# A four-layer decoder trunk on one core: attention steps reordered, low halves of weights moved from GpSimd to VectorE, and the last layer's down products turned

## The chip, the cores and the metric

The kernel runs on one core of a Trainium2 chip. A core has a matrix engine (TensorE), three engines for everything else (VectorE, ScalarE, GpSimd), a fifth one (SyncE) that only issues transfers, and DMA engines that move data between the chip's memory (HBM) and the core's working memory (SBUF). TensorE's results go to eight banks of accumulators (PSUM), from which VectorE and ScalarE read. The metric is the device time of one execution, in microseconds (us).

## The reference

A trunk of four pre-norm residual layers works on 256 tokens of 1024 features, in float32. Each layer adds a token mixer, then a SwiGLU feed-forward step with 2816 hidden features; a last RMS norm with its own gain ends it.

```python
for i in range(4):
    h = h + mixer[i % 3](rms_norm(h, norm_mix[i]))
    a = rms_norm(h, norm_ffn[i])
    h = h + (silu(a @ w_gate[i]) * (a @ w_up[i])) @ w_down[i]
return rms_norm(h, norm_final)
```

Layers 0 and 3 use native sparse attention (NSA): 16 query heads in 4 groups; keys and values exist in three kinds (for compressed blocks, for selected blocks, for a window). With 256 tokens every block is selected and the window reaches over all tokens, so the second and third kind are two full causal attentions. The compressed kind runs its keys and values through a small network (two products with a GELU between) and has 15 blocks. The three results are weighted by sigmoid gates, projected from the same input, and summed. Layer 1 uses MoBA, which with one block of 256 tokens is plain causal attention with 16 heads. Layer 2 is a gated convolution over three tokens between two projections.

## The kernel before

**Precision.** Matrix products run in a rounded float32 form. A number is split in two: a high half (a copy rounded to that form, `whi` for weights) and a low half (the number minus its high half, `wlo`). A product is three matmuls: high by high, high by low, low by high (`mm3`, L132 to L137; `group_wide` L139 does the first two at once with 512 columns, L155, and the third with 256, L159).

**The weight stream.** `stream()` (L884) lists all weights in the order in which the steps use them, and `tiles` packs them on the host into parts of eight 128x128 tiles (512 KB). `take` (L118) hands out tiles in that order and makes the parts ahead: up to five parts, the current one included (`AHEAD`), are loaded (four buffers `raw`), and split by `split_part` (L94) into five buffers each of `whi` and `wlo`. ScalarE makes the high half in one copy (L111). The low half is one subtraction of 128x1024 on VectorE or four of 128x256 on GpSimd (L115). Which engine makes it is written in the table `LO` (L42): a word per step, read cyclically by the part's number, `v` for VectorE, `p` for GpSimd. Steps that are not in the table, the convolution and the feed-forward steps among them, use VectorE. The weights of the compression network (step `F`) are used whole, in plain float32, and loaded straight into a `whi` buffer.

**The mixers as lists of steps.** `NSA_ORDER` and `MOBA_ORDER` (L39 to L41) are words that `steps` (L396) calls one by one. A, K, q, k: projections with the features on the partitions (A: four at once, raw compressed keys and values; K: keys; each `project`, L255, of 24 matmuls per 128 features). G: projection of the gates, which are transposed to tokens on the partitions right away (`put_gates`, L541, L545). V: values with tokens on the partitions (`values`, L359, 48 matmuls of 512 columns for each call). F, E, C, D: compression, its GELU, its keys and values. c, t: compressed scores with their softmax, and their transposes. For each pair of heads s, T, P: scores (L698 in NSA, L444 in MoBA) and softmax (`softmax`, L377: row minima `mn` of the negated, masked scores on VectorE L386, exponentials on ScalarE L389, division and gate on GpSimd L393), transposes (L718, L459) with a split of the result (`split`, L182: high half on ScalarE L184, low half on VectorE L185), and the products with the values (L735, L473). Step numbers count up unless a number is written.

**Accumulators.** The eight banks are three pools: A with four, B with three, C with one. Projections, values and scores use A (a pair of NSA heads takes three), transposes B.

**Feed-forward.** `ffn` (L285) has the tokens on the partitions for gate and up (L345 to L347), turns the hidden rows over 32x32 transposes on VectorE (L304) and small transfers, and splits them (L321). `out_proj` (L268) then computes the down products (and the mixers' output projections) with features on the partitions, four tiles of 128 features at once and then four single ones, adds them to `h` (L275, L276), and prepares the next norm: `prep` (L188) scales by the gain and splits, squares on ScalarE (L211) and sums squares on GpSimd (L213). The norm's factor is applied later, from sums that TensorE makes (`rms_sums` L226) and a power on GpSimd (`rms_tokens` L234, L239).

**The end.** For the last norm (number 8) `prep` makes rows scaled by the final gain, `turn_rows` (L217, L223) transposes them on TensorE beside the down products, and `run` scales them by the norm's factor (L871, L873) and stores four pieces of 128x512 over SyncE's queue (L874).

**Order on the engines.** The program is written on tiles; the framework's planner decides each engine's order of instructions from the written order, as priorities, and its own estimate of when things are ready, and sets the waits.

## Time and profile before

| | us |
|---|---|
| median of 3 runs | 1271.21 (1270.64 to 1273.55) |
| profiled execution | 1274.58 |
| its span, first instruction to last | 1272.8 |
| TensorE busy | 1239.8 |
| VectorE, ScalarE, GpSimd busy | 861.0, 686.5, 334.0 |
| mean granted TensorE clock, share of 2.4 GHz | 0.995 |

In the rows, PE is TensorE (PEld its weight loads), DVE VectorE, ACT ScalarE, POOL GpSimd, SPq SyncE's queue; L115 is line 115 of the kernel. Matmuls overlap: one of 512 columns is shown with some 390 ns, while the next may start earlier, so a stretch is read by its count and length. A releaser (`<-`) is what ended an engine's idle time. For GpSimd the kernel's lines show as one row where an instruction follows the other (x8: eight of them).

### The profile page before, as it was taken

What the parts mean: (1) busy time and instruction counts of PE and PEld (TensorE: products, weight loads), DVE (VectorE), ACT (ScalarE), POOL (GpSimd) and SP (SyncE); (2) the same over time, 40 slices, a digit from 0 to 9 for tenths busy, and PEclk for the clock granted to TensorE, in tenths of its full rate; (3) what the DMA queues carried; (4) which work ended last, traced back from release to release, by engine and by line L of the source; (5) the groups of instructions that cost most, each with busy time, mean ns of one, the idle gap of its engine ahead of it and who ended that gap; (6) DMA issues with size and microseconds to landing.
All of it is one profiled execution on the core that took longest, in us unless ns stands there. A gap on an engine that the chain in (4) does not pass through costs nothing.

```text
span 1272.8 us, 20178 instructions
## 1 busy us (share of the span) xinstructions
PE 1239.8 (97%) x7108; PEld 1082.7 (85%) x7108; DVE 861.0 (68%) x1621; ACT 686.5 (54%) x1231; POOL 334.0 (26%) x492
## 2 busy tenths in 40 slices
PE   8998999999998999999999999999999989999997
PEld 8977888888898888888899988888899878888886
DVE  7578785665648785656758786565746797756663
ACT  5578754554456754545434444454446796545542
POOL 3577610000467310000113110000346865000011
PEclk9999999999999999999999999999999999999999
DMA  8732166767554336776665656776655312677761
GB/s 278 244 110 64 42 208 199 243 198 228 181 180 124 112 120 197 232 212 205 222 189 171 199 183 196 216 220 213 205 183 199 115 36 69 205 221 217 227 210 51
DMA packets 91445, 226.73 MB, mean 178 GB/s; under 512 B 17488, under 2 KB 38352, under 8 KB 91344
## 3 DMA queue, kind: packets, MB, share of 16 engines
q1 hardware_dynamic: 91200, 225.41, 57.0%
q8 instruction: 56, 0.92, 0.3%
q14 instruction: 45, 0.37, 0.1%
q10 hardware_dynamic: 144, 0.04, 0.0%
HBM read 212.81 MB, written 1.05 MB: 168 GB/s over the span
## 4 chain that ended last, share of the span: by engine, by line
PE 85%; DVE 6%; ACT 4%; issue 3%; POOL 1%; DMA 0%; POOLq 0%; SPq 0%; DVEq 0%; ACTq 0%
PE psA L155 15%; PE psA L159 8%; PE psB L345 6%; PE psB L347 6%; PE psB L346 6%; PE psA L346 5%; PE psA L345 5%; PE psA L347 5%; PE psA L135 4%; PE psA L136 4%; PE psA L137 4%; PE psB L581 2%; PE psB L155 2%; PE psC L347 2%; PE psC L345 2%
## 5 line engine op out<-in xcount | busy, mean ns | idle before, releaser
L111 ACT CAST whi<-raw 128x1024 fp32r<-128x1024 f32 (+1 forms) x390 | 405.2, 1040 | 451.4 <-PE psC L347 97.4
L115 DVE TENSOR_TENSOR wlo<-raw,whi 128x1024 fp32r<-128x1024 f32 (+1 forms) x338 | 410.9, 1221 | 265.2 <-ACT whi L111 246.2
L155 PE MATMUL psA<-ff,whi 128*128 128x512 f32 x840 | 228.5, 393 | 0.0
L213 POOL TENSOR_TENSOR ssq<-ssq,row 128x256 f32<-128x256 f32 x48 | 45.7, 951 | 546.9 <-issue 398.6
L115 POOL TENSOR_TENSOR wlo<-raw,whi 128x256 fp32r<-128x256 f32 x208 | 157.8, 792 | 61.8 <-ACT whi L111 52.0
L155 PEld LDWEIGHTS psA<-ff,whi 128*128 128x128 f32 x840 | 149.4, 189 | 23.9
L135 PE MATMUL psA<-at,whi 128*128 128x256 f32 x536 | 153.9, 287 | 0.0
L137 PE MATMUL psA<-at,wlo 128*128 128x256 f32 x536 | 152.9, 285 | 0.0
L136 PE MATMUL psA<-at,whi 128*128 128x256 f32 x536 | 152.7, 285 | 0.0
L345 PE MATMUL psB<-whi,at 128*128 128x512 f32 x352 | 137.4, 390 | 0.0
L347 PE MATMUL psB<-whi,at 128*128 128x512 f32 x352 | 137.0, 389 | 0.0
L346 PE MATMUL psB<-wlo,at 128*128 128x512 f32 x352 | 136.9, 389 | 0.0
L159 PEld LDWEIGHTS psA<-ff,wlo 128*128 128x128 f32 x840 | 123.1, 190 | 10.9
L159 PE MATMUL psA<-ff,wlo 128*128 128x256 f32 x840 | 129.7, 282 | 0.0
L136 PEld LDWEIGHTS psA<-at,whi 128*128 128x128 f32 x536 | 103.6, 193 | 0.6
L135 PEld LDWEIGHTS psA<-at,whi 128*128 128x128 f32 x536 | 103.6, 193 | 0.5
L137 PEld LDWEIGHTS psA<-at,wlo 128*128 128x128 f32 x536 | 103.5, 193 | 0.0
L345 PE MATMUL psA<-whi,at 128*128 128x512 f32 x256 | 99.6, 389 | 0.0
L346 PE MATMUL psA<-wlo,at 128*128 128x512 f32 x256 | 99.6, 389 | 0.0
L347 PE MATMUL psA<-whi,at 128*128 128x512 f32 x256 | 99.6, 389 | 0.0
L389 ACT ACTIVATE pr<-pr,mn 128x128 f32<-128x128 f32 (+1 forms) x160 | 71.4, 450 | 13.7 <-DVE mn L386 12.8
L347 PEld LDWEIGHTS psB<-whi,at 128*128 128x128 f32 x352 | 66.1, 188 | 13.9
(214 smaller groups left out, 2037.6 us busy)
## 6 DMA issues: line engine op xcount, KB each, us to landing
raw<-in_w SPq DMA_DIRECT2D x384, 512.0 KB, 4.2
pt<-pt SPq DMA_DIRECT2D x320, 32.0 KB, 3.0
wf<-in_w SPq DMA_DIRECT2D x16, 512.0 KB, 4.3
h<-in_xt SPq DMA_DIRECT2D x4, 256.0 KB, 5.3
raw<-in_w SPq DMA_DIRECT2D x4, 256.0 KB, 5.3
pt<-pt SPq DMA_DIRECT2D x64, 16.0 KB, 3.1
out<-ff SPq DMA_DIRECT2D x4, 256.0 KB, 2.5
w<-in_w SPq DMA_DIRECT2D x2, 256.0 KB, 3.8
```

Of the source, the lines that this page charges most:

```text
L111: nc.scalar.copy(hi[:, c], src[:, c])
L115: eng.tensor_tensor(out=lo[:, d], in0=src[:, d], in1=hi[:, d].bitcast(F32), op=OP.subtract)
L135: mm(out, wt[0], act[0], start=first, stop=False)
L136: mm(out, wt[0], act[1], start=False, stop=False)
L137: mm(out, wt[1], act[0], start=False, stop=last)
L155: mm(outs[o], w[0], acts[k].rearrange("p i s -> p (i s)"), start=(k == 0), stop=(k == n - 1))
L159: mm(outs[o][:, :S], w[1], acts[k][:, 0, :], start=False, stop=False)
L213: (nc.gpsimd if norm else nc.vector).tensor_tensor(out=self.ssq, in0=self.ssq, in1=sq, op=OP.add)
L345: mm(o, a[:, 0, s], hi, start=(k == 0), stop=False)
L346: mm(o, a[:, 0, s], lo, start=False, stop=False)
L347: mm(o, a[:, 1, s], hi, start=False, stop=(k == KT - 1))
L389: nc.scalar.activation(pr[:, c], pr[:, c], AF.Exp, bias=mn[:, j:j + 1], scale=-1.0, accum_out=den[:, j:j + 1])
```

## The change

Both lists of steps have another order, and a new step `g` holds the transposes of the gates, apart from their projection. `LO` keeps four entries; a second table, `HI`, puts some high halves on VectorE (`a` is ScalarE). The low half of the NSA keys' second copy moves from GpSimd to VectorE. In the last layer `finish` takes the place of `out_proj`: tokens on the partitions, four banks for all 1024 features, the residual brought in by products with the identity, the final gain broadcast over the partitions and applied by VectorE, squares summed by ScalarE out of the banks, and two queues for the stores. Of the last four feed-forward tiles each bank is finished by itself, token half by token half. The stream then holds this layer's down weights by rows of 1024. `PROJ_BANKS` and `PR` carry the values that stood in the code before; the host's layout adds the broadcast gain and drops it from the table of gains.

```diff
@@ -36,14 +36,18 @@
 ROW_BUFS = 7
 PT_BUFS = 5
 PS_BUFS = {"A": 4, "B": 3, "C": 1}
-NSA_ORDER = ("A K0 q K3 F q F K1 F q F E G K2 q C c0 s D q s T t0 V q s T P q P s T P q T s "
-             "c1 s P T t1 s P T s P T P T P").split()
-MOBA_ORDER = ("V0 k k V1 q q k k s s q q T s k q s P T k T P q s P T q q P T k s T k s P s P T T P P").split()
-LO = {"V": "vp", "q": "vp", "nsa_out": "p", "moba_out": "vvvp", "G": "vvp", "K": "vp", "A": "vp", "moba_q": "p", "moba_V": "vp", "moba_k": "vvvp"}
-PIECES = 4
+NSA_ORDER = ("A q K q F K3 F F K1 F E G K g q q D C c s q s V t T q P s T q s P T q T c s s P T P s t P s T T "
+             "P T P P").split()
+MOBA_ORDER = ("k V k k q q q s s V T q k s s P k T q k T P q s q P T q P T k s k T s s P T P P T P").split()
+LO = {"nsa_out": "p", "moba_out": "vp", "G": "p", "A": "p"}
+HI = {"A": "v", "G": "ava", "K": "ava", "moba_out": "v"}
 OUT_BANKS = "AAAB"
 CMP_BANK = "B"
 GELU = "vector"
+PIECES = 4
+PROJ_BANKS = "AABB"
+PR = ["gpsimd"]
+KEY_LO = ["vector", "vector"]
 CONE = "vector"
 NPAIR = 8
 NCMP = 15
...
@@ -103,12 +107,13 @@
         src = self.raw.pop(q)
         hi = self.operands.tile([P, PART * P], F32R, tag="whi", name=f"whi{q}", bufs=W_BUFS)
         lo = self.operands.tile([P, PART * P], F32R, tag="wlo", name=f"wlo{q}", bufs=W_BUFS)
-        lo_eng = LO.get(self.names[q], "v")
+        lo_eng, hi_eng = (e.get(self.names[q], d) for e, d in ((LO, "v"), (HI, "a")))
         eng = {"p": nc.gpsimd, "v": nc.vector}[lo_eng[q % len(lo_eng)] if q >= 4 else "v"]
+        copy = {"a": nc.scalar.copy, "v": nc.vector.tensor_copy}[hi_eng[q % len(hi_eng)] if q >= 4 else "a"]
         n = PART * P // (2 if q < 4 else 1)
         for o in range(0, PART * P, n):
             c = slice(o, o + n)
-            nc.scalar.copy(hi[:, c], src[:, c])
+            copy(hi[:, c], src[:, c])
             m = n // (PIECES if eng is nc.gpsimd else 1)
             for b in range(o, o + n, m):
                 d = slice(b, b + m)
...
@@ -192,17 +197,11 @@
         g = self.gain[:, norm, k:k + 1]
         if k == 0:
             self.at = [None] * KT
-            self.scaled_rows = []
             self.ssq = None
-        if norm < 8:
-            a = self.operands.tile([P, 2, S], F32R, tag="at", name=self.uid("at"), bufs=8)
-            nc.vector.tensor_scalar(a[:, 0, :], h, g, None, op0=OP.mult)
-            nc.vector.scalar_tensor_tensor(a[:, 1, :], h, g, a[:, 0, :].bitcast(F32), op0=OP.mult, op1=OP.subtract)
-            self.at[k] = a
-        else:
-            hg = self.row()
-            nc.vector.tensor_scalar(hg, h, g, None, op0=OP.mult)
-            self.scaled_rows.append(hg)
+        a = self.operands.tile([P, 2, S], F32R, tag="at", name=self.uid("at"), bufs=8)
+        nc.vector.tensor_scalar(a[:, 0, :], h, g, None, op0=OP.mult)
+        nc.vector.scalar_tensor_tensor(a[:, 1, :], h, g, a[:, 0, :].bitcast(F32), op0=OP.mult, op1=OP.subtract)
+        self.at[k] = a
         if k == 0:
             self.ssq = self.sb([P, S], "ssq", bufs=1)
             nc.scalar.activation(self.ssq, h, AF.Square)
...
@@ -214,18 +213,9 @@
         else:
             self.sq = sq
 
-    def turn_rows(self, k):
-
-        if k == 0:
-            self.turned = [[self.bank(c) for _ in range(NT)] for c in "AB"]
-        for t in range(NT):
-            c = slice(k % 4 * P, (k % 4 + 1) * P)
-            self.nc.tensor.transpose(self.turned[k // 4][t][:, c], self.scaled_rows[k][:, t * P:(t + 1) * P],
-                                     self.ident)
-
     def rms_sums(self):
         nc = self.nc
-        pt = self.sums = self.bank("C" if self.norm == 8 else "A" if self.norm % 2 else "B")
+        pt = self.sums = self.bank("A" if self.norm % 2 else "B")
         for t in range(NT):
             c = slice(t * P, (t + 1) * P)
             nc.tensor.matmul(pt[:, t:t + 1], self.ssq[:, c], self.ones, start=True, stop=False)
...
@@ -276,9 +266,6 @@
                 self.nc.vector.tensor_tensor(out=h, in0=p[:, S:], in1=h, op=OP.add)
             for i in range(n):
                 self.prep(m + i, norm)
-            if norm == 8:
-                for k in range(max(m - 4, 0), m + n - 4):
-                    self.turn_rows(k)
             m += n
 
 
...
@@ -348,7 +335,60 @@
             if self.rstd is None:
                 self.rms_tokens()
             hidden(banks, n)
-        self.out_proj(hs, norm + 1)
+        (self.out_proj if norm < 7 else self.finish)(hs, norm + 1)
+
+
+    def finish(self, hs, norm):
+        nc = self.nc
+        mm = nc.tensor.matmul
+        g = self.sb([P, D], "pt", bufs=PT_BUFS)
+        nc.sync.dma_start(g, self.ap["gfin"])
+        banks = [[self.bank(c) for _ in range(2)] for c in "AB"]
+        for t in range(NT):
+            for k in range(KT):
+                mm(banks[t][k // 4][:, k % 4 * P:(k % 4 + 1) * P], self.h[k][:, t * P:(t + 1) * P], self.ident,
+                   start=(k % 4 == 0), stop=False, skip_group_check=True)
+
+        def products(t, k, halves, w):
+            s = slice(t * P, (t + 1) * P)
+            for hf in halves:
+                o, (hi, lo) = banks[t][hf], w[hf]
+                mm(o, hs[k][:, 0, s], hi, start=False, stop=False, skip_group_check=True)
+                mm(o, hs[k][:, 0, s], lo, start=False, stop=False, skip_group_check=True)
+                mm(o, hs[k][:, 1, s], hi, start=False, stop=(k == FT - 1), skip_group_check=True)
+
+        ss = self.sb([P, 2 * NT], "ss", bufs=1)
+
+        def scale(t):
+            xs = []
+            for hf in range(2):
+                x, y = (self.sb([P, 512], "pr", bufs=PR_BUFS) for _ in range(2))
+                nc.scalar.activation(x, banks[t][hf], AF.Square, accum_out=ss[:, 2 * t + hf:2 * t + hf + 1])
+                nc.vector.tensor_tensor(out=y, in0=banks[t][hf], in1=g[:, hf * 512:(hf + 1) * 512], op=OP.mult)
+                xs.append(y)
+            v, r = self.sb([P, 1], "var"), self.sb([P, 1], "rstd")
+            nc.vector.tensor_tensor(out=v, in0=ss[:, 2 * t:2 * t + 1], in1=ss[:, 2 * t + 1:2 * t + 2], op=OP.add)
+            nc.vector.tensor_scalar(v, v, 1.0 / D, EPS, op0=OP.mult, op1=OP.add)
+            nc.gpsimd.tensor_tensor(out=r, in0=v, in1=self.mhalf[:, :1], op=OP.pow)
+            for hf, y in enumerate(xs):
+                o = self.ff([P, 512], F32)
+                if hf:
+                    nc.scalar.activation(o, y, AF.Identity, scale=r)
+                else:
+                    nc.vector.tensor_scalar(o, y, r, None, op0=OP.mult)
+                (nc.scalar if hf else nc.sync).dma_start(self.ap["out"][t * P:(t + 1) * P, hf * 512:(hf + 1) * 512], o)
+
+        cut = FT - 4
+        for k in range(cut):
+            w = [self.take(4) for _ in range(2)]
+            for t in range(NT):
+                products(t, k, range(2), w)
+        ws = [[self.take(4) for _ in range(2)] for _ in range(cut, FT)]
+        for t in range(NT):
+            for hf in range(2):
+                for k in range(cut, FT):
+                    products(t, k, [hf], ws[k - cut])
+            scale(t)
 
 
     def scaled(self, p):
...
@@ -531,16 +571,20 @@
                     r, o = slice(i * DH, (i + 1) * DH), slice((1 - i) * DH, (2 - i) * DH)
                     nc.scalar.copy(kk[r, 0, b, :], f[r])
                     nc.scalar.copy(kk[o, 0, b, :], f[r])
-                    for eng, d in ((nc.vector, r), (nc.gpsimd, o)):
+                    for eng, d in zip((getattr(nc, e) for e in KEY_LO), (r, o)):
                         eng.tensor_tensor(out=kk[d, 1, b, :], in0=f[r], in1=kk[r, 0, b, :].bitcast(F32),
                                           op=OP.subtract)
             return put
 
         gates = self.sb([P, NT, 48], "gates", bufs=1)
 
+        scaled = []
+
         def put_gates(p):
-            f = self.scaled(p)
-            pg = self.bank("B")
+            scaled.append(self.scaled(p))
+
+        def turn_gates(_):
+            f, pg = scaled[0], self.bank("B")
             for t in range(NT):
                 nc.tensor.transpose(pg[:, t * P:(t + 1) * P], f[:, t * P:(t + 1) * P], self.ident)
             nc.scalar.activation(gates, pg[:, :S].rearrange("p (t c) -> p t c", t=NT)[:, :, 80:], AF.Exp, scale=-1.0)
...
@@ -857,21 +901,6 @@
             if i == 0:
                 self.pad_keys()
             self.ffn(2 * i + 1)
-        self.begin(8)
-        for k in range(4, KT - 1):
-            self.turn_rows(k)
-        self.rms_sums()
-        self.turn_rows(KT - 1)
-        self.rms_tokens()
-        for t in range(NT):
-            for hf in range(2):
-                o = self.ff([P, 512], F32)
-                src, r = self.turned[hf][t], self.rstd[:, t:t + 1]
-                if hf:
-                    nc.scalar.activation(o, src, AF.Identity, scale=r)
-                else:
-                    nc.vector.tensor_scalar(o, src, r, None, op0=OP.mult)
-                nc.sync.dma_start(ap["out"][t * P:(t + 1) * P, hf * 512:(hf + 1) * 512], o)
         assert self.pos == self.nblk * PART
 
 
...
@@ -916,7 +945,10 @@
         for g in range(0, FT, 4):
             n = min(4, FT - g) * P
             s.append(("ffn", "ffn_gate_up", i, np.concatenate([r(g * P, n), r(DFF + g * P, n)])))
-        s += out("ffn_w_down", i, "down")
+        if i < LAYERS[-1]:
+            s += out("ffn_w_down", i, "down")
+        else:
+            s.append(("down", "ffn_w_down", i, r(0, D)))
     return s
 
 
```

## Rows read from the trace of the kernel before

**Rows 1.** The page's busy times, TensorE's and its weight loads' lines.

```profile
PE 1239.8 (97%) x7108; PEld 1082.7 (85%) x7108; DVE 861.0 (68%) x1621; ACT 686.5 (54%) x1231; POOL 334.0 (26%) x492
```

**Rows 2.** Busy time by stage (stretch from:to in us from the span's start and its length, then busy us and instructions of each engine, the mean granted TensorE clock as a share of 2.4 GHz, the share of time that the DMA engines were busy, GB/s): first layer's attention and the head of its output projection, second layer's attention, short convolution, fourth layer's attention, last feed-forward stage and end; and TensorE's first matmul in order of time (start, length, engine, line, operation, out<-in, shapes, count, idle time before it and what ended it).

```profile
0.00:149.00 149.00, 135.12 (x938) 121.56 (x939) 112.45 (x342) 107.94 (x284) 90.47 (x147) 0.99 0.45 149
...
346.00:454.00 108.00, 103.77 (x679) 93.20 (x678) 70.79 (x168) 68.70 (x156) 59.39 (x93) 0.98 0.45 139
...
651.00:721.00 70.00, 70.00 (x586) 70.00 (x585) 52.47 (x84) 27.84 (x32) 17.24 (x22) 1.00 0.61 180
...
925.00:1066.00 141.00, 133.31 (x948) 120.68 (x947) 98.39 (x309) 101.11 (x268) 88.21 (x136) 0.99 0.37 120
1066.00:1273.00 207.00, 199.59 (x1000) 169.48 (x998) 126.91 (x175) 93.01 (x123) 21.13 (x25) 0.99 0.60 185
...
5.81 1.22 PE L177 MATMUL psA<-at,whi 128*128 128x256 f32 x4 [5.81 <-ACT whi L111]
```

**Rows 3.** TensorE's instructions in order of time at its longer stalls (columns as in the last row above; the bracket holds the idle time and its releaser).

```profile
56.97 0.44 PE L545 MATMUL psB<-ident,row 128*128 128x128 f32 x2 [0.81 <-DVE row L356]
...
109.40 0.73 PE L742 MATMUL psC<-pt,ff 128*128 128x512 f32 x1 [2.06 <-ACT pr L389]
...
403.58 0.47 PE L451 MATMUL psA<-keys,ff 128*128 128x512 f32 x1 [1.03 <-DVE mn L386]
...
411.51 0.33 PE L466 MATMUL psB<-ident,pr 128*128 128x128 f32 x1 [2.19 <-DVE pt L185]
...
974.21 0.44 PE L545 MATMUL psB<-ident,row 128*128 128x128 f32 x2 [0.81 <-DVE row L356]
...
996.71 0.60 PE L369 MATMUL psA<-whi,at 128*128 128x512 f32 x1 [1.81 <-DVE mn L386]
...
1027.30 0.47 PE L742 MATMUL psC<-pt,ff 128*128 128x512 f32 x1 [1.35 <-ACT pr L389]
```

**Rows 4.** Busy time of three stretches that begin with a long stall (columns as by stage; the share behind POOL is the granted clock).

```profile
107.00:115.00 8.00, 5.94 (x31) 5.28 (x31) 7.10 (x33) 5.68 (x19) 5.10 (x10) 0.79 0.24 68
411.00:419.00 8.00, 7.44 (x41) 6.60 (x41) 6.16 (x14) 5.34 (x13) 1.62 (x4) 0.79 0.59 197
994.00:1003.00 9.00, 7.19 (x27) 5.45 (x27) 7.41 (x28) 7.20 (x24) 4.65 (x9) 0.81 0.18 59
```

**Rows 5.** VectorE's and GpSimd's instructions in order of time, at some of these places (first start, time from the first start to the last end, line, count).

```profile
104.46 2.00 DVE L185 TENSOR_TENSOR ff<-row,ff 128x256 fp32r<-128x256 f32 x1 [0.42 <-ACT ff L184]
...
103.35 2.81 POOL L115 TENSOR_TENSOR wlo<-raw,whi 128x256 fp32r<-128x256 f32 x4
...
396.03 5.57 DVE L185 TENSOR_TENSOR ff<-row,ff 128x256 fp32r<-128x256 f32 x1 [0.23 <-ACT ff L184]
...
395.72 5.61 POOL L115 TENSOR_TENSOR wlo<-raw,whi 128x256 fp32r<-128x256 f32 x8
...
122.35 0.61 DVE L658 TENSOR_TENSOR row<-row,cmx 128x256 f32<-128x256 f32 x1
...
120.75 4.20 POOL L393 TENSOR_SCALAR pr<-pr,rc,gates 128x128 f32<-128x128 f32 x8 [1.48 <-DVE rc L391]
```

**Rows 6.** Groups of instructions by line and shape, whole span (out<-in, shapes, count | busy us, mean ns of one | idle time of the engine before them and what ended it).

```profile
L115 DVE TENSOR_TENSOR wlo<-raw,whi 128x1024 fp32r<-128x1024 f32 x330 | 406.0, 1234 | 265.2 <-ACT whi L111 246.2 <-DMA pt<-pt 16.7 <-issue 0.3
...
L115 POOL TENSOR_TENSOR wlo<-raw,whi 128x256 fp32r<-128x256 f32 x208 | 157.8, 792 | 61.8 <-ACT whi L111 52.0 <-issue 7.1 <-DVE row L591 1.5
...
L185 DVE TENSOR_TENSOR ff<-pt,ff 128x256 fp32r<-128x256 f32 x88 | 31.5, 417 | 0.0
...
L581 PE MATMUL psB<-pt,wf 128*128 128x80 f32 x256 | 29.6, 273 | 0.0
...
L185 DVE TENSOR_TENSOR ff<-row,ff 128x256 fp32r<-128x256 f32 x32 | 24.3, 759 | 4.1 <-ACT ff L184 3.9
```

**Rows 7.** The start and the end of the last down products in order of time (all engines), two groups by line of other stages, and a stretch of the first feed-forward stage with TensorE alone (busy us, instructions, granted clock, DMA).

```profile
1201.27 0.84 PE L155 MATMUL psA<-ff,whi 128*128 128x512 f32 x3
...
1263.13 0.40 PE L155 MATMUL psA<-ff,whi 128*128 128x512 f32 x1
...
1265.90 0.16 DVE L237 TENSOR_SCALAR var<-psC 128x2 f32<-128x2 f32 x1 [0.98 <-PE psC L232]
1266.14 0.70 POOL L239 TENSOR_TENSOR rstd<-var,mhalf 128x2 f32<-128x2 f32 x1 [8.27 <-DVE var L237]
...
1266.87 1.41 DVE L873 TENSOR_SCALAR ff<-psA,rstd 128x512 f32<-128x512 f32 x2 [0.81 <-POOL rstd L239]
1267.59 1.81 SPq L874 DMA_DIRECT2D out<-ff  x4
...
L389 ACT ACTIVATION_READ_ACCUMULATOR pr<-pr,mn 128x1 f32 x160 | 30.4, 190 | 0.0
...
L302 ACT ACTIVATE pr<-psB,rstd 128x512 f32<-128x512 f32 x24 | 16.3, 685 | 3.9 <-PE psB L347 3.2 <-POOL rstd L239 0.7
...
190.00:280.00 90.00, 90.00 (x399) 1.00 0.69 212
```

**Rows 8.** Busy time of the two middle stretches of attention and of the first layer's projections and compression (columns as by stage).

```profile
60.00:140.00 80.00, 72.91 (x456) 61.56 (x455) 66.19 (x246) 67.90 (x212) 60.06 (x100) 0.98 0.25 78
350.00:446.00 96.00, 91.85 (x620) 83.45 (x620) 63.96 (x157) 61.71 (x147) 56.95 (x90) 0.98 0.45 138
12.00:60.00 48.00, 47.19 (x403) 46.99 (x403) 32.78 (x62) 26.05 (x45) 24.42 (x31) 1.00 0.78 261
```

13 lines of the change are left out of this document (7 added, 6 removed).

## The prediction

> **What bounds the kernel now.** I read the page's busy times first, then a table of all engines by stage, then the TensorE instructions in time order wherever TensorE sat idle, then what VectorE and GpSimd did just before. TensorE is busy for 1239.8 us of 1272.8 [rows 1], and its idle time lies in four places only [rows 2]: 13.9 us in the first layer's attention (149.00 - 135.12, of which 5.8 us pass before the first matmul, row at 5.81), 4.2 us in the second layer's, 7.7 us in the fourth layer's, 7.4 us at the very end. The short convolution runs at 70.00 of 70.00, and the feed-forward stages between are as full. So the time is the matmul stream plus stalls in the three attention stages plus a tail; the other engines matter only where they make TensorE wait.
>
> Seven stalls stand out [rows 3]: 0.81 us at 56.97 and again at 974.21, where the transposes of the gates (L545) wait for VectorE's row L356; 2.06 at 109.40; 1.03 at 403.58; 2.19 at 411.51; 1.81 at 996.71; 1.35 at 1027.30. After three of them the granted clock falls to 1.2 GHz for a while: its mean is 0.79, 0.79 and 0.81 over 8, 8 and 9 us [rows 4], which at the two levels 1.2 and 2.4 GHz is 0.21 x 8 = 1.7 us lost each time. Each of these three drops follows an idle of 1.8 us or more, and the shorter idles of rows 3 bring none.
>
> Behind the five longer stalls stands VectorE, and behind VectorE, GpSimd. At 396.03 one subtraction of 128x256 (L185, both inputs in SBUF) took 5.57 us, within 395.72 to 401.33, where GpSimd made eight pieces of low halves in a row [rows 5]. At 104.46 another took 2.00, up to 0.3 us after a run of four ended.  By the groups [rows 6] the same subtraction out of the moved rows (ff<-pt), when GpSimd does nothing, takes 0.417. These instructions are followed on VectorE's queue by the row minima (L386, mn) that the exponentials and the release of the score banks wait for, and this is what the waits at 403.58 and 996.71 (DVE mn) and at 109.40 and 1027.30 (ACT pr, itself fed by mn) name.
>
> **The change part by part.** Terms in us; the profiled execution took 1274.58 (span 1272.8 and 1.8 around it), 0.27% above the median 1271.21; I apply the sum to the latter.
>
> *The last layer's down products.* Before: from 1201.27 to the end of the last product, 1263.13 + 0.40, that is 62.3 [rows 7]. After: 22 k x 2 token tiles x 2 halves x 3 = 264 matmuls of 512 columns. The feed-forward stage runs the same form with 399 in 90.00, 0.226 each: 59.7. The residual comes in by 16 plain f32 matmuls with the identity. Plain f32 ones show as two records (256 records of L581 for 128 in the code, 29.6 busy): 16 x 2 x 0.116 = 3.7. Sum 63.4, +1.1. The eight pairs of transposes (L223) and the sums of squares go; most of these lie inside the 62.3 or in the chain below.
> The chain behind the last product: before, 1272.8 - 1263.5 = 9.3 (two adds into h, a square, sums on TensorE, the power on GpSimd, four scalings on two engines, four stores issued one behind the other by SP from 1267.59 on). After: 0.05 release, a square of 128x512 out of PSUM (0.685 as L302 of that size) and its accumulator's read 0.19, an add and a scaling of one column (0.16 each as L237), the power 0.70, one scaling 0.70, and some 0.3 for five hand-overs: 2.95. Then the stores: the last of four was issued some 0.45 x 3 after 1267.59, near 1268.95, and the span ends 3.85 later; two queues with one store each have the same 3.85. That is 6.8, so -2.5. Net **-1.4** (bounds -3.0, if the residual's matmuls fill gaps, and +1.0, if the last square queues behind other work). Inputs are not late: the last hidden rows are wanted at k = 20 of 22, after 20 x 12 x 0.226 = 54 us, where the old order wanted them in its first pass over four banks, within about 31 us (88 of 176 tiles in 62.3). The 512 KB of gains and the last weights come well ahead in a stage where DMA is at 0.6 [rows 2].
>
> *The gates' transposes* come a key projection later (24 matmuls behind the projection, where 0.81 is missing): both stalls go, **-1.6** (bounds -1.6 to 0).
>
> *Low halves.* GpSimd made 208 pieces, 52 parts [rows 6]; after the change it makes 16 of the NSA output projections, 4 of the MoBA one, 2 of the gates and 4 of the fourth layer's first projection: 26. VectorE gets the other 26 x 1.234 = 32.1, 16 key halves at 0.417, the subtraction of that length (6.7), and about 15 high halves. No row shows a copy of 128x1024 on VectorE: a bound above is four times the 0.417 subtraction of 128x256, 1.7, one below a quarter of that; I take 1.2, as the subtraction of that size (L115): 18. Against this goes the stretching: L185 ff<-row is 0.342 above ff<-pt over 32 [rows 6], 11 us, with the half-width subtractions not counted. ScalarE loses the 15 high halves.
> Where it lands: in 60:140 VectorE is busy 66.2 of 80, in 350:446 64.0 of 96 [rows 8]. Six parts and two key halves add 8.2 in the first, and as much in the fourth layer; 14 parts less 2, and 8 high halves, add 24.4 in the second. No wait of TensorE for a low half shows now: the parts are made up to four ahead, and a part lasts 24 matmuls of some 0.12 (the convolution's 586 in 70.00 [rows 2]), 2.9 us. The work is hidden by VectorE's idle time as long as there is some; near 93% of a stretch there will be little, and I charge **+3.0** for new waits (bounds 0 and the slow rival below).
> What it gives: the five stalls sum to 8.44, and the clock after three of them to 5.1, together 13.5. Not all is GpSimd's: at 996.71 the values' matmuls wait for score banks as well, and at 411.51 the transposes wait for VectorE's evacuation of their bank (DVE pt), behind low halves of its own. I take two thirds, **-9.0** (bounds 0 and -13.5).
>
> A rule speaks for less. The Trainium skill, "SBUF — State Buffer", section "Who interferes with whom", says that a VectorE instruction with two SBUF inputs and a GpSimd one that reads SBUF exclude each other, and that the later waits until the other has finished. By that a subtraction would be held by one piece at a time, an estimate of 0.8, not by eight; then little of the five stalls would be GpSimd's. The trace differs: 5.57 us, over eight pieces [rows 5]. Beside the normalising multiplications (L393) the trace does agree: L658 took 0.61 inside a run of eight that lasted 4.20. I go by the rows.
>
> *The new orders.* They move the value projection in NSA right behind the second scores and in MoBA behind the first key projection. Each projection keeps its 24 or 48 matmuls; filler is only moved. The order on each engine is made by the framework's planner, so I can't read it off the diff. The values wait for score banks already (1.81 at 996.71), and the scores' minima still have to come first: bounds -3.5 (the stall of 1.81 and its 1.7 of clock go) and +5.7 (4 us more idle, about two parts' low halves and two pairs of heads' minima in front, with one more drop of the clock). The nearest row is the old stall, which stays: I take 0. Two compression steps now follow each other, whose parts come by SP's queue straight into the operand buffers: 4 parts of 512 KB in 64 matmul records, 7.4 us, are 283 GB/s, where 12:60 moves 261 with the DMA engines busy 0.78 of it [rows 8]; full use would be 335, the buffers ahead cover more than the landing, and the rest of SP's queue stays in its order: 0, at most +1 in each of two layers.
>
> Sum: -1.4 - 1.6 - 9.0 + 3.0 = -9.0; 1271.2 - 9.0 = **1262**.
>
> **The rivals.**
> (a) *The stalls move on.* Chains of scores, exponentials, transposes are as long as before; what GpSimd no longer holds, the exponentials do (ScalarE 67.9 of 80 in 60:140 [rows 8]). Then the five stalls and the charge both drop out, and one gate stall comes back elsewhere: -1.4 - 0.8 = -2.2, **1269**. For it: ScalarE as full as VectorE. Against: the held instruction of 5.57. The rule above leads here too.
> (b) *All goes.* The five stalls, their clock, the gates and the tail, and about 2 more of the short waits of transposes on GpSimd's L393: -13.5 - 1.6 - 1.4 - 2 = -18.5, **1253**. For it: GpSimd has only L393 to do in the middle of the attention. Against: VectorE has less idle time than now.
> (c) *VectorE becomes the bound* of the attention stages: low halves come later than the matmuls that use them. Added are 8.2, 8.2 and 24.4, 40.8 together; if a quarter falls on TensorE's path and nothing is won back from the five stalls, +10.2 - 1.4 - 1.6 = +7.2, **1278**. It decides from the point where TensorE waits for wlo, of which there is no row now. For it: (66.2 + 8.2) of 80 is 93%. Against: the stretching, 11 us and more, is given back just there.
>
> **How the numbers follow.** Forecast 0.46 (own range 1257 to 1267), (a) 0.20, (b) 0.18, (c) 0.16. This kernel's measurement can tell about 0.2%, 2.5 us, from no change. (a) at 1269 lies at that edge: 0.14 of it within, 0.06 beyond. Faster 0.46 + 0.18 + 0.06 = 0.70; same 0.14; slower 0.16. The range 1252 to 1272 leaves out most of (c) and the far side of (b).
>
> **What would show it.** Right: no VectorE subtraction over 1.5 us in MoBA; TensorE's idle in the three attention stages falling from 13.9, 4.2 and 7.7 by about 6 together; fewer than three drops of the clock; no wait on L545; an end of about 6.8 us behind the last product. Wrong: TensorE waiting for wlo from VectorE, values' matmuls waiting longer for mn with a clock drop behind them, or the same number of drops at other places.

## The result and the profile after

The changed kernel takes 1260.79 us (median of 4 runs, 1260.33 to 1261.87), the kernel before beside it 1272.37 (1270.64 to 1273.55): a ratio of 0.9911, 95% interval 0.9894 to 0.9928, so 11.6 us less. Forecast were 1262 and a range of 1252 to 1272. The profiled run took 1260.33, span 1258.4.

The page's busy times after, to lay beside [rows 1]:

```profile
PE 1232.9 (98%) x7028; PEld 1075.7 (85%) x7028; DVE 877.1 (70%) x1661; ACT 670.2 (53%) x1216; POOL 239.6 (19%) x367
```

GpSimd gives up 94 us of work, and VectorE, which takes most of it over, is only 16 us busier; some 6 of what it saves come from the new end (35.8 us of VectorE work in the last stage before, 29.9 after). TensorE is idle for 1258.4 - 1232.9 = 25.5 us, where it was idle for 33.0; its busy time fell by 6.9 too, part of it clock (0.995 in the mean before, 0.997 after). The same three attention stretches as in [rows 2], and the last one to the new end (columns as there):

```profile
0.00:149.00 149.00, 137.86 (x962) 124.90 (x963) 115.40 (x360) 110.17 (x287) 67.84 (x117) 0.99 0.45 150
346.00:454.00 108.00, 106.34 (x704) 96.06 (x704) 84.11 (x199) 64.11 (x154) 32.42 (x52) 1.00 0.46 137
925.00:1066.00 141.00, 135.37 (x951) 121.86 (x950) 109.93 (x342) 102.40 (x273) 66.28 (x108) 1.00 0.38 120
1066.00:1258.40 192.40, 185.75 (x844) 154.38 (x842) 110.25 (x137) 86.16 (x112) 4.03 (x6) 0.99 0.62 193
```

TensorE's idle time in them is 11.1, 1.7 and 5.6 us, against 13.9, 4.2 and 7.7. The longest waits that are left, from TensorE's instructions in order of time:

```profile
64.37 0.38 PE L140 MATMUL psA<-at,whi 128*128 128x256 f32 x1 [0.87 <-DVE row L396]
...
78.94 0.47 PE L409 MATMUL psA<-whi,at 128*128 128x512 f32 x1 [1.07 <-DVE mn L426]
...
116.82 0.33 PE L767 MATMUL psB<-ident,pr 128*128 128x128 f32 x1 [0.81 <-POOL pr L433]
...
972.23 0.38 PE L140 MATMUL psA<-at,whi 128*128 128x256 f32 x1 [0.85 <-DVE row L396]
...
986.80 0.47 PE L409 MATMUL psA<-whi,at 128*128 128x512 f32 x1 [1.07 <-DVE mn L426]
```

None of the seven stalls of [rows 3] stands in this list; no idle is as long as the 1.35 to 2.19 us of the four longest. What is late next are waits that the new order brings: the value projection (L409) for the minima in both NSA layers, 1.07 each, and the products that now stand behind the scores (L140) for VectorE's row. One drop of the clock is left of three; it follows the wait of 0.81 at 116.82. The stretch around it (the granted clock stands behind POOL):

```profile
115.00:123.00 8.00, 6.57 (x28) 4.26 (x27) 6.44 (x34) 7.03 (x29) 7.36 (x14) 0.79 0.20 67
```

The groups by line that answer to [rows 6] (low halves now L120, the subtraction L190, the keys' halves L575, high halves L116):

```profile
L120 DVE TENSOR_TENSOR wlo<-raw,whi 128x1024 fp32r<-128x1024 f32 x356 | 435.9, 1229 | 267.4 <-ACT whi L116 252.3 <-DMA pt<-pt 12.0
...
L120 POOL TENSOR_TENSOR wlo<-raw,whi 128x256 fp32r<-128x256 f32 x104 | 77.9, 786 | 80.5 <-ACT whi L116 41.0 <-DVE whi L116 22.0 <-PE psA L493 8.2
...
L190 DVE TENSOR_TENSOR ff<-row,ff 128x256 fp32r<-128x256 f32 x32 | 15.5, 486 | 6.3 <-ACT ff L189 6.0
L575 DVE TENSOR_TENSOR keys<-row,keys 64x256 fp32r<-64x256 f32 x32 | 13.4, 418 | 0.5
L116 DVE CAST whi<-raw 128x1024 fp32r<-128x1024 f32 x15 | 12.9, 858 | 6.7 <-PE psA L141 2.5 <-PE psA L160 1.8 <-PE psB L625 1.7
```

The counts are those that the prediction read off the diff: 26 parts left on GpSimd (104 pieces), 26 more on VectorE, 15 high halves. The subtraction of two SBUF tiles fell from 759 to 486 ns. The end, to lay beside [rows 7], in order of time (all engines):

```profile
1188.17 1.50 PE L349 MATMUL psA<-ident,h 128*128 128x128 f32 x12
...
1251.37 0.39 PE L358 MATMUL psB<-whi,ff 128*128 128x512 f32 x1
1251.79 0.60 ACT L366 ACTIVATE pr<-psB 128x512 f32<-128x512 f32 x1 [1.27 <-PE psB L358]
...
1253.63 0.55 POOL L372 TENSOR_TENSOR rstd<-var,mhalf 128x1 f32<-128x1 f32 x1 [4.98 <-DVE var L371]
1254.21 0.72 ACT L376 ACTIVATE ff<-pr,rstd 128x512 f32<-128x512 f32 x1 [1.74 <-POOL rstd L372]
...
1254.97 0.34 ACTq L379 DMA_DIRECT2D out<-ff  x1
```

The products run from 1188.17 to 1251.76, 63.6 us (forecast 63.4), and 6.6 us lie behind them (forecast 6.8).

### The profile page after: what moved, and what is told of

It is laid out like the page before. It is cut to its first block, busy times and chain, and to the rows that moved or that the text cites. A ratio compares the mean times of both kernels' runs of the same rounds, so it can differ in the third digit from the quotient of the medians.

```text
span 1258.4 us, 19867 instructions
## 1 busy us (share of the span) xinstructions
PE 1232.9 (98%) x7028; PEld 1075.7 (85%) x7028; DVE 877.1 (70%) x1661; ACT 670.2 (53%) x1216; POOL 239.6 (19%) x367
## 4 chain that ended last, share of the span: by engine, by line
PE 86%; ACT 6%; DVE 4%; POOL 2%; DMA 1%; SPq 1%; issue 1%; POOLq 0%; ACTq 0%; DVEq 0%
PE psA L160 12%; PE psA L164 6%; PE psB L332 6%; PE psB L333 6%; PE psB L334 6%; PE psA L333 5%; PE psA L332 5%; PE psA L334 5%; PE psA L140 4%; PE psA L141 4%; PE psA L142 4%; PE psB L625 2%; ACT pr L429 2%; PE psB L160 2%; PE psC L333 2%; PE psC L332 2%
## 5 line engine op out<-in xcount | busy, mean ns | idle before, releaser
L116 ACT CAST whi<-raw 128x1024 fp32r<-128x1024 f32 (+1 forms) x375 | 389.2, 1039 | 463.0 <-DMA raw<-in_w 101.3
L120 DVE TENSOR_TENSOR wlo<-raw,whi 128x1024 fp32r<-128x1024 f32 (+1 forms) x364 | 440.9, 1217 | 267.4 <-ACT whi L116 252.3
L160 PE MATMUL psA<-ff,whi 128*128 128x512 f32 x686 | 187.1, 394 | 0.4 <-DVE ff L526 0.4
L140 PE MATMUL psA<-at,whi 128*128 128x256 f32 x536 | 153.7, 287 | 1.7 <-DVE row L396 1.7
L160 PEld LDWEIGHTS psA<-ff,whi 128*128 128x128 f32 x686 | 121.6, 189 | 19.7 <-DVE ff L526 0.6
L212 POOL TENSOR_TENSOR ssq<-ssq,row 128x256 f32<-128x256 f32 x42 | 38.9, 927 | 395.7 <-issue 265.4
L164 PEld LDWEIGHTS psA<-ff,wlo 128*128 128x128 f32 x686 | 100.6, 190 | 9.2
L164 PE MATMUL psA<-ff,wlo 128*128 128x256 f32 x686 | 106.0, 282 | 0.0
L140 PEld LDWEIGHTS psA<-at,whi 128*128 128x128 f32 x536 | 102.5, 191 | 2.8 <-DVE row L396 2.6
L120 POOL TENSOR_TENSOR wlo<-raw,whi 128x256 fp32r<-128x256 f32 x104 | 77.9, 786 | 80.5 <-ACT whi L116 41.0
L433 POOL TENSOR_SCALAR pr<-pr,rc,gates 128x256 f32<-128x256 f32 (+1 forms) x128 | 72.1, 577 | 65.6 <-ACT pr L429 42.3
```

Of the source, the lines that this page charges most:

```text
L116: copy(hi[:, c], src[:, c])
L120: eng.tensor_tensor(out=lo[:, d], in0=src[:, d], in1=hi[:, d].bitcast(F32), op=OP.subtract)
L140: mm(out, wt[0], act[0], start=first, stop=False)
L160: mm(outs[o], w[0], acts[k].rearrange("p i s -> p (i s)"), start=(k == 0), stop=(k == n - 1))
L164: mm(outs[o][:, :S], w[1], acts[k][:, 0, :], start=False, stop=False)
L212: (nc.gpsimd if norm else nc.vector).tensor_tensor(out=self.ssq, in0=self.ssq, in1=sq, op=OP.add)
```

## The experiments

One table carries all of them: stage lengths of each profiled run, read off the first and last matmuls of the four feed-forward stages. They are the first layer's attention up to the first of these; the first down products with the second layer's attention (MoBA); the third layer's down products with the fourth layer's attention; and the end. The rest (convolution 154.2, four times 120.4) is the same in all within 1.0 us of before. Ratios are to the kernel before, run on the same chip beside them. A stage length comes from one profiled run, and these differ in their drops of the clock. Before has a drop in each of the three attention stages; e3_tail, whose attention is the same, has one in the first stage alone. Over 346:454 its granted clock is 1.00 where [rows 2] have 0.98, and its MoBA and fourth layer's stages are 1.4 us shorter. So 1.4 us of a difference in one of these stages can be the clock.

| kernel | first layer | MoBA | fourth layer | end | ratio (95% interval) |
|---|---|---|---|---|---|
| before | 164.1 | 184.3 | 216.7 | 71.7 | 1 |
| after | 160.3 | 178.7 | 212.5 | 70.4 | 0.9911 (0.9894 to 0.9928) |
| e1_lo: tables alone | 160.5 | 178.3 | 212.9 | 71.7 | 0.9905 (0.9891 to 0.9918) |
| e2_order: orders alone | 164.3 | 179.1 | 216.2 | 71.7 | 0.9967 (0.9955 to 0.9979) |
| e3_tail: end alone | 164.5 | 182.9 | 215.3 | 70.7 | 0.9986 (0.9978 to 0.9995) |
| e4_nolo: orders and end | 164.7 | 178.8 | 218.0 | 70.5 | 0.9962 (0.9950 to 0.9975) |
| e5_lo_tail: tables and end | 160.8 | 178.2 | 212.6 | 70.5 | 0.9894 (0.9874 to 0.9913) |
| e6_low_only | 162.3 | 178.7 | 214.4 | 71.7 | 0.9920 (0.9902 to 0.9938) |
| e7_moba_low | 163.0 | 178.6 | 216.1 | 71.7 | 0.9953 (0.9936 to 0.9970) |
| e8_pieces8 | 161.7 | 179.0 | 217.9 | 71.7 | 0.9952 (0.9934 to 0.9971) |
| e9_pieces1 | 167.3 | 180.8 | 218.3 | 71.7 | 1.0021 (1.0012 to 1.0030) |
| e10_nsa_v | 163.9 | 179.0 | 215.2 | 70.7 | 0.9956 (0.9943 to 0.9970) |
| e11_old_nsa_v | 163.8 | 178.6 | 216.0 | 70.5 | 0.9944 (0.9932 to 0.9956) |
| e12_pr_both | 172.9 | 178.1 | 223.8 | 70.5 | 1.0071 (1.0058 to 1.0085) |

### Which part of the change carries it

Theory G: GpSimd's runs of low halves hold VectorE, so the tables carry the gain. Theory O: the orders do. Tables alone (e1_lo), on the kernel before:

```diff
-LO = {"V": "vp", "q": "vp", "nsa_out": "p", "moba_out": "vvvp", "G": "vvp", "K": "vp", "A": "vp", "moba_q": "p", "moba_V": "vp", "moba_k": "vvvp"}
+LO = {"nsa_out": "p", "moba_out": "vp", "G": "p", "A": "p"}
+HI = {"A": "v", "G": "ava", "K": "ava", "moba_out": "v"}
+KEY_LO = ["vector", "vector"]
```

> The kernel before with only the tables of the change (low halves, high halves, key halves on VectorE); orders, gates and the end as before. Theory G (GpSimd's runs of pieces hold VectorE's two-SBUF-input subtractions, and that is what stalls TensorE): 5 to 7 us less than before (-9 and +3 of the prediction), no subtraction L185 over 1.5 us in MoBA, at most one drop of the clock. Theory O (the orders do it): within 1.5 us of before, the long waits still there. Theory J (only both together): less than 3 us gained here, and less than 3 with the orders alone.

Measured 1261.72 against 1273.89, 12.2 less: the whole gain, without the orders and the turned end, and twice what was expected of the tables. Its trace shows which stalls go. Both gates' waits, both of MoBA and the values' wait at 996.71 are gone, 0.81 x 2 + 1.03 + 2.19 + 1.81 = 6.65 us; TensorE's idle time in the three stages falls by 1.4 + 2.9 + 2.4. The other two stay. The first of them, from TensorE, VectorE and GpSimd in order of time:

```profile
106.90 0.47 PE L745 MATMUL psC<-pt,ff 128*128 128x512 f32 x1 [2.08 <-ACT pr L392]
...
101.95 2.01 DVE L188 TENSOR_TENSOR ff<-row,ff 128x256 fp32r<-128x256 f32 x1 [0.43 <-ACT ff L187]
...
100.85 2.82 POOL L118 TENSOR_TENSOR wlo<-raw,whi 128x256 fp32r<-128x256 f32 x4
```

The stretch around it (the granted clock stands behind POOL):

```profile
104.50:112.50 8.00, 5.92 (x43) 5.25 (x42) 7.58 (x35) 6.85 (x22) 5.10 (x10) 1.00 0.23 68
```

The run of four is a part of the NSA output projection, which the table leaves on GpSimd. The idle of 2.08 us is as long as the 2.06 of [rows 3], and yet no drop of the clock follows in this run: 1.00 against 0.79 [rows 4].

Orders and the gates' step alone (e2_order):

```diff
-NSA_ORDER = ("A K0 q K3 F q F K1 F q F E G K2 q C c0 s D q s T t0 V q s T P q P s T P q T s "
+NSA_ORDER = ("A q K q F K3 F F K1 F E G K g q q D C c s q s V t T q P s T q s P T q T c s s P T P s t P s T T "
...
-MOBA_ORDER = ("V0 k k V1 q q k k s s q q T s k q s P T k T P q s P T q q P T k s T k s P s P T T P P").split()
+MOBA_ORDER = ("k V k k q q q s s V T q k s s P k T q k T P q s q P T q P T k s k T s s P T P P T P").split()
...
-            f = self.scaled(p)
+            scaled.append(self.scaled(p))
```

> The kernel before with only the two new orders and the gates' transposes as a step of their own; tables and end as before. Theory G: 1 to 2.5 us less than before, from the gates alone; VectorE's subtractions of 2 to 5 us beside GpSimd's runs remain. Theory O: 7 to 11 us less. Theory J: less than 3 us.

Measured 1270.05, 3.8 less, and all of it in MoBA (184.3 to 179.1), not at the gates as expected. In the NSA layers new stalls take the place of the old, the longest of them:

```profile
64.82 0.58 PE L629 MATMUL psB<-w,row 128*128 128x128 f32 x1 [2.82 <-DVE row L622]
```

With the tables beside it (the profile after) this one is gone.

The turned end alone (e3_tail: the changed kernel with the old orders and the old tables) and with the orders (e4_nolo: the changed kernel with the old tables):

```diff
-LO = {"nsa_out": "p", "moba_out": "vp", "G": "p", "A": "p"}
-HI = {"A": "v", "G": "ava", "K": "ava", "moba_out": "v"}
+LO = {"V": "vp", "q": "vp", "nsa_out": "p", "moba_out": "vvvp", "G": "vvp", "K": "vp", "A": "vp", "moba_q": "p", "moba_V": "vp", "moba_k": "vvvp"}
+HI = {}
...
-KEY_LO = ["vector", "vector"]
+KEY_LO = ["vector", "gpsimd"]
```

> The changed kernel with the orders, the gates and the tables put back: only the last layer's down products and the end are new. All theories: 1.0 to 1.8 us less than before (term of -1.4); the end after the last product 6.8 us instead of 9.3, the products with the residual 1.1 us longer. If the term was wrong: 0 or a loss.

> The changed kernel with only the tables put back: new orders, gates apart, new end. Theory G: 3 us less than before (-1.4 and -1.6), so 8 to 9 us slower than the changed kernel. Theory O: within 2 us of the changed kernel. Theory J: 3 to 5 us less than before.

Measured 1271.91 (2.0 less) and 1269.38 (4.5 less). The end's own stage is 1.0 to 1.3 us shorter wherever it is turned. The changed kernel with the old orders (e5_lo_tail: only NSA_ORDER and MOBA_ORDER set back, the gates' step behind G):

> The changed kernel with the old orders (gates turned right behind their projection): tables and end of the change. The tables alone gave 12.2 us and the end alone 2.0. If the new orders add nothing to the tables: 14 us less than before, so 1 to 2 us faster than the changed kernel. If the orders still carry their 1.8 of the gates: 11 to 12 us less.

Measured 1261.06 against 1274.34, 13.3 less; its interval overlaps the changed kernel's. So the orders add nothing on top of the tables that these runs can tell (0.9911 with them, 0.9894 without). Alone the three parts give 12.2 + 3.8 + 2.0 = 18.0, together 11.6: tables and orders mend the same MoBA stage, and neither can do it twice.

### Which part of the tables

e6_low_only has the new LO alone (HI empty, the keys' second halves left on GpSimd); e7_moba_low keeps the old table but for its MoBA projections:

```diff
-LO = {"V": "vp", "q": "vp", "nsa_out": "p", "moba_out": "vvvp", "G": "vvp", "K": "vp", "A": "vp", "moba_q": "p", "moba_V": "vp", "moba_k": "vvvp"}
+LO = {"V": "vp", "q": "vp", "nsa_out": "p", "moba_out": "vvvp", "G": "vvp", "K": "vp", "A": "vp"}
```

> The kernel before with the new table of low halves only; high halves all on ScalarE and the second key halves on GpSimd as before. If the low halves are the whole effect of the tables: 11 to 12.5 us less than before. If the high halves of the projections and the key halves have their own share: 8 to 10 us less, with waits of TensorE on ScalarE's high halves, or on the keys (0.99 us at 980 before), left.

> The kernel before with the low halves of the second layer's projections alone on VectorE (14 parts). Theory G: the second layer's attention alone gets shorter, by 5 to 6 us, no subtraction of 5.57 us there, no drop of the clock there; the NSA stages as before within 0.5. If the saving of the tables lies mostly in the NSA layers: 0 to 3 us.

Measured 1264.59 (9.8 less) and 1267.99 (6.4 less). MoBA's low halves are worth half of the gain, and the stage table puts 5.7 of it into that stage, 4.3 against e3_tail's stage without a drop of the clock. By the medians the NSA layers' low halves add some 3.4, the high halves and keys another 2.4; for the last the intervals overlap (0.9920 against 0.9905), so it is not shown.

### How GpSimd holds VectorE

The prediction read from one instruction of 5.57 us that VectorE is held until GpSimd's whole run ends. The same work in pieces of other sizes, on the kernel before:

```diff
-PIECES = 4
+PIECES = 8
```

> The kernel before with each low half on GpSimd cut in eight pieces of 128x128 instead of four of 128x256. If a subtraction on VectorE is held for one piece at a time: none over 1.2 us beside GpSimd's runs, and 2 to 6 us less than before. If it is held for the run of pieces: subtractions of 2 to 6 us remain, and the time is within 2 us of before or longer, since the runs last longer by the pieces' fixed cost.

> The kernel before with each GpSimd low half of 128x1024 as one subtraction instead of four of 128x256 (PIECES = 1), everything else as before. GpSimd's runs stay as long (about 2.8 us for one part, 5.6 us for two in a row), only the seams between pieces go. Theory G1 (a VectorE subtraction of two SBUF tiles is held until GpSimd's whole run of back-to-back pieces ends): holds of 5.5 us and 2.0 us stand as before, the time within 0.2% of the kernel before. Theory G2 (held until the one GpSimd instruction in progress ends, and finer pieces shorten it): holds go up to about 2.8 us, one instruction's length, and more of the short ones are seen; the time no better than before, up to 6 us worse, the mirror of the run with pieces of 128x128.

With eight pieces GpSimd is busier, and yet the kernel takes 1268.49, 5.9 less; with one (PIECES = 1) it takes 1276.16, 2.5 more. GpSimd's group at eight:

```profile
L115 POOL TENSOR_TENSOR wlo<-raw,whi 128x128 fp32r<-128x128 f32 x416 | 199.0, 516 | 39.9 <-ACT whi L111 31.0 <-issue 7.5 <-POOL keys L535 1.1
```

Two of VectorE's longest subtractions there, each with the GpSimd run beside it, in order of time:

```profile
1015.89 1.81 DVE L185 TENSOR_TENSOR ff<-row,ff 128x256 fp32r<-128x256 f32 x1 [0.94 <-ACT ff L184]
...
1014.85 2.57 POOL L115 TENSOR_TENSOR wlo<-raw,whi 128x128 fp32r<-128x128 f32 x6
...
371.56 3.30 DVE L115 TENSOR_TENSOR wlo<-raw,whi 128x1024 fp32r<-128x1024 f32 x1 [6.53 <-ACT whi L111]
...
370.79 2.98 POOL L115 TENSOR_TENSOR wlo<-raw,whi 128x128 fp32r<-128x128 f32 x7
```

With one, GpSimd's group:

```profile
L115 POOL TENSOR_TENSOR wlo<-raw,whi 128x1024 fp32r<-128x1024 f32 x52 | 126.3, 2433 | 78.6 <-ACT whi L111 69.2 <-issue 6.4 <-PE psA L707 1.2
```

A hold there under a single GpSimd instruction (two subtractions in one row, 3.04 us; in the changed kernel such a pair takes 0.87), and two stalls of TensorE:

```profile
63.89 3.04 DVE L561 TENSOR_TENSOR ff<-row,ff 64x256 fp32r<-64x256 f32 x2
...
64.30 2.36 POOL L115 TENSOR_TENSOR wlo<-raw,whi 128x1024 fp32r<-128x1024 f32 x1
...
96.71 0.50 PE L707 MATMUL psA<-keys,ff 128*128 128x512 f32 x1 [2.53 <-DVE row L356]
...
997.97 0.47 PE L369 MATMUL psA<-whi,at 128*128 128x512 f32 x1 [2.47 <-DVE mn L386]
```

No hold with one piece is longer than one GpSimd instruction; there are many of that length, and the 5.57 and 2.00 are gone. So of the two theories recorded with this run, G2, held for the single instruction, is the usual case, and G1, held for the whole run, the exception. A count over the trace of before says how rare: 227 VectorE instructions began inside a GpSimd piece, 48 were held by over 0.1 us against the median of their kind, and only 4 of these across a seam between two pieces (its end, less that median, lies behind the end of the piece in which it began), the 5.57 and the 2.00 among them. By the same count there are six with eight pieces, the longest the one at 371.56, and none with one. This is what the Trainium skill, "SBUF — State Buffer", section "Who interferes with whom", states, a lock for the length of the other instruction; here it covers 44 of 48 holds and every one of the run with one piece. What lets a run of pieces keep VectorE out across its seams, no run shows.

A long hold does not by itself cost time. In e2_order, which keeps the old tables, four subtractions in MoBA take 4.00 us, the first of them 2.65, beside a run of eight:

```profile
366.88 4.00 DVE L412 TENSOR_TENSOR keys<-row,keys 64x256 fp32r<-64x256 f32 x4
...
363.61 5.63 POOL L115 TENSOR_TENSOR wlo<-raw,whi 128x256 fp32r<-128x256 f32 x8
```

Yet its MoBA stage is 179.1, as short as with the tables, and that of e8_pieces8, with the hold at 371.56, is 179.0. What a hold costs depends on whether TensorE has other work just then.

### One step further

If GpSimd's low halves cost that much, the last ones should be worth moving too. The changed kernel with the NSA output projections' low halves on VectorE (e10_nsa_v), the same with the old orders (e11_old_nsa_v), and e10 with half of the softmax's normalising multiplications moved as well (e12_pr_both):

```diff
-LO = {"nsa_out": "p", "moba_out": "vp", "G": "p", "A": "p"}
+LO = {"moba_out": "vp", "G": "p", "A": "p"}
...
-PR = ["gpsimd"]
+PR = ["gpsimd", "vector"]
```

> The changed kernel with the low halves of nsa_out's weights on VectorE too (the table's entry nsa_out: p left out); A and G stay on GpSimd, moba_out stays shared. In the changed kernel TensorE's transposes behind layers 0's and 3's scores still wait for GpSimd's normalise (pr, 0.81 and 0.53 us the longest, about 4.5 us over the kernel). Theory G (GpSimd's low halves cost, by holding VectorE or by standing ahead of the normalise on GpSimd): these waits shrink below 0.4 us each and the time is 1 to 3 us under the changed kernel's, ratio to the kernel before 0.989 to 0.990. Rival (VectorE takes the load in the stage where it is busiest, 115 of 149 us): the values' waits for mn (1.07 us each) grow by more than the pr waits shrink, and the time is 1 to 4 us above the changed kernel's.

> The changed kernel with the old orders of the attention steps and with nsa_out's low halves on VectorE. With the old orders and the new tables the stalls of 2.08 us at 106.90 and 1.35 us at 1014.25 (scores wait for ScalarE's pr) remained, and a VectorE subtraction of 2.01 us stood beside a GpSimd run of 2.82 us ahead of the first. Theory G: that run is a part of nsa_out, so with it on VectorE both stalls go or fall under 0.7 us, and the time is 2 to 4 us under that of the old orders with the new tables (1261.06), ratio to the kernel before 0.987 to 0.989. Rival (these stalls belong to the old order of the steps): both remain within 0.3 us of what they were and the time is 1260 to 1263 us.

> As the run with nsa_out's low halves on VectorE (new orders), and besides the softmax's normalise takes turns between GpSimd and VectorE (PR = gpsimd, vector). On GpSimd one of 128x256 takes 621 ns, so a group of four takes 2.5 us after the reciprocal. Theory G with GpSimd as the late engine: the transposes' waits for pr go below 0.2 us and the time is 1 to 3 us under that run's. Rival (VectorE is by now the late engine): VectorE's share rises over 72%, the waits for mn and pt grow, and the time is equal or up to 3 us above it.

Measured 1267.10, 1266.08 and 1282.68, against 1273.63 before. In e10 and e12 the rival holds, by more than it said: 0.45% above the changed kernel by the ratios, 5.7 us, then another 15.6. In e11 neither side comes out whole: the same move costs 0.50% against e5_lo_tail, so its time is above both forecasts, and of its two stalls one shrank by 0.6. The stretch 60 to 140 of after, e10 and e12, in this order (columns as in [rows 2]; before is in [rows 8]):

```profile
60.00:140.00 80.00, 75.15 (x478) 63.81 (x476) 68.50 (x258) 69.65 (x216) 54.26 (x92) 0.98 0.23 76
```

```profile
60.00:140.00 80.00, 72.49 (x453) 61.24 (x452) 71.95 (x257) 67.44 (x211) 42.68 (x67) 0.98 0.21 68
```

```profile
60.00:140.00 80.00, 68.17 (x414) 56.33 (x414) 72.54 (x255) 60.58 (x185) 20.18 (x30) 0.96 0.22 69
```

VectorE's third number goes from 68.50 to 71.95 and 72.54 of 80, and TensorE's first falls from 75.15 to 72.49 and 68.17. VectorE is hardly held any more: the longest excess of any of its instructions in e10 is 0.6 us. I had read the waits for GpSimd's normalise as GpSimd's low halves standing in the way; in e10 GpSimd has 64 pieces fewer, and TensorE's waits for it are more (wait, total us, times, longest us; after, then e10):

```profile
PE psB L767 <- POOL pr L433: 1.8, 3, 0.8
PE psB L768 <- POOL pr L433: 1.7, 4, 0.6
```

```profile
PE psB L767 <- POOL pr L433: 1.8, 3, 0.7
PE psB L768 <- POOL pr L433: 3.1, 8, 0.6
```

GpSimd's group, by line, after and in e10:

```profile
L433 POOL TENSOR_SCALAR pr<-pr,rc,gates 128x128 f32<-128x128 f32 x64 | 33.6, 533 | 65.6 <-ACT pr L429 42.3 <-DVE rc L431 22.0 <-PE psB L768 1.0
```

```profile
L433 POOL TENSOR_SCALAR pr<-pr,rc,gates 128x128 f32<-128x128 f32 x64 | 37.9, 600 | 98.5 <-ACT pr L429 42.8 <-DVE rc L431 35.0 <-PE psA L142 19.6
```

GpSimd stands idle ahead of these multiplications, in e10 35.0 us of it for VectorE's reciprocal, so no backlog of its own stands ahead of them. But they also last longer, 600 ns against 533, because the hold works the other way too: a multiplication that overlaps a low half on VectorE can take 1.3 to 1.7 us in place of some 0.5. Of 160 multiplications 3 last over 1 us in the kernel before, 9 after and 17 in e10, every one beside a low half on VectorE. The longest stand in e12, here two multiplications beside three low halves in a row:

```profile
86.54 3.25 POOL L433 TENSOR_SCALAR pr<-pr,rc,gates 128x128 f32<-128x128 f32 x2 [1.26 <-DVE rc L431]
...
87.17 3.69 DVE L120 TENSOR_TENSOR wlo<-raw,whi 128x1024 fp32r<-128x1024 f32 x3
```

So two causes stand side by side, a VectorE that is busier and hands its results on later, and low halves on VectorE that now hold GpSimd. No run separates them.

In e11 the two stalls of the old order stay (1.49 and 1.47 us, where they were 2.08 and 1.35), with no run of low halves on GpSimd beside them: for the larger part they belong to the order. No version that was run beats the changed kernel beyond the intervals.

## Why the prediction was right, and where its steps were not

The time and the sign came out, and so did four of the signs that the prediction named: idle in the three attention stages falls by 7.4 us, one drop of the clock is left, no transpose of the gates waits, and the end takes 6.6 us. The sum is near in part by luck. It has the low halves some 6 us too small; against that, the gates' 1.6 is no gain of its own, and the orders, set to 0, may cost 2 on top of the tables (0.9911 against 0.9894, with overlapping intervals).

- *The end*, -1.4: right to 0.2 in each half. The stage shortens by 1.27; e3_tail gives 0.14% (0.05 to 0.22%), 1.8 us.
- *Low halves*, -9.0 and +3.0, net -6.0: right mechanism, mis-sized. e1_lo gives -12.2, of which 6.65 are the stalls listed there and some 4 the clock. The high halves cost 0.86 us each, not 1.2. The charge of +3.0 for VectorE's load isn't visible at this load: VectorE is busy for 68.5 of 80 in the first layer's middle stretch, where I had (66.2 + 8.2). Over the whole first layer's stage it goes from 124.77 in 164.11 to 125.92 in 160.34, since shorter instructions give back most of what the parts cost; with the tables alone it is 130.30. A charge comes one step further on, where 16 parts more cost 5.7.
- *Which stalls are GpSimd's.* I named the two at 109.40 and 1027.30 with the other three and took two thirds of all. e1_lo sorts them: three of the five go (5.03 us of 8.44, close to two thirds), and those two stay. The held subtraction of 2.00 in front of the first is at most a part of its cause: in e11 the run of GpSimd is gone and 1.49 of the 2.08 us remain. They go with the new order.
- *The gates' stalls*, -1.6, I put down to the later transposes. They go with the tables alone as well: L548, as L545 is numbered there, starts without a wait. What was late was VectorE's row, not the place of the step.

```profile
56.69 0.44 PE L548 MATMUL psB<-ident,row 128*128 128x128 f32 x2
```

- *The orders*, 0 in the sum: 3.8 alone, nothing on top of the tables (e5_lo_tail). Right for the change as a whole, for a reason that I didn't give: they reach the stall that the tables remove.
- *The clock*, 5.1 us for three drops: too much for the time as it is measured. Nor does a drop go by the length of the idle, as the three cases of before suggest: after, it follows a wait of 0.81, while idles of 2.08 (e1_lo) and of 2.22 at 411.83 (e3_tail) bring none. The drops don't come in every run. In the comparisons, five runs of the kernel before at a mean granted clock of 0.999 span 1269.1 to 1269.6, nineteen at 0.995 span 1271.9 to 1274.8; so the drops of such a run are worth about 4. At 0.999 the changed kernel spans 1259.0 and e1_lo 1259.6, one run each: some 10 of the 11.6 remain without any help of the clock.
- *The rule that I weighed and set aside* was the better description of the holds (e9_pieces1). It did not lead to rival (a), as I had it: few holds are long, and the gain is there all the same. That the many short holds make it up in the NSA layers is argued, not shown; in MoBA the 14 parts on GpSimd cost the stage 4.3 to 5.7 us with the old order (e7_moba_low), the long hold and the short ones together.

Rival (a), the stalls move on: refuted, since idle time falls by 7.5. Rival (b), all goes: what it counted on top, the waits on L433, is still there. Rival (c), VectorE becomes the bound: false here; e10 and e12 come out its way, with the second cause above unseparated. Its point of decision was wrong: TensorE never waits for a low half there. It waits for minima and rows from VectorE and for GpSimd's multiplications, whose reciprocals come from VectorE too.

## What to carry to other kernels

Moving work off an engine whose instructions hold another's can cost the receiver less than the durations say, as the waits inside its own instructions shrink: some 51 us of instructions moved to VectorE by the tables, and it was 26 busier (e1_lo, 886.6 against 861.0). Look for the same instruction with two mean times (759 here, 417 there) before adding durations, and look on both engines: what is moved can hold the giver in turn. The gain ended abruptly: with VectorE busy for 86% of the tightest stretch the move paid, at 90% the next 16 parts cost 5.7 us, by VectorE's load or by the holds on GpSimd. Where two edits mend one stall, price them one at a time and don't add: 18.0 us of single gains were 11.6 together.

## What was not expected of the hardware

Splitting GpSimd's work finer made it slower (199.0 us against 157.8) and the kernel faster, by 5.9 us. Of the 48 holds counted above, 44 end no later than the next seam, so more seams let VectorE in sooner. One piece of 128x1024 is the cheapest for GpSimd (126.3) and the worst for the kernel.

The idle of TensorE alone doesn't decide on its clock: after 2.06 us the granted clock fell in the profile of before, after 2.08 us at the same place it stayed at 1.00 in e1_lo, and in the profile after it fell behind waits of 0.81 and less. What decides was not tried.

VectorE copies 128x1024 from f32 in 858 ns, where its subtraction of that size takes 1229: I had taken the subtraction's price for both.
